# A two-layer diffusion backbone on one core: the FFN norm, the operand splits and the operand sums are emitted in turn with plain FFN tiles, the first two inner tiles are interleaved, and the next layer's modulation and norm are spread over the down phase

## The chip, the cores and the metric

The kernel runs on one core of a Trainium2 chip. The metric is the device time of one execution in microseconds (us), the median over several runs; less is better.

## The reference, cut to what matters

1024 latent tokens and 256 context tokens of width 1024 pass two layers. Everything is float32. What the change touches is the second half of a layer, its channel mixing, and the start of the next layer.

```python
def rms_norm(x, g, eps=1e-6):
    y = x * lax.rsqrt(jnp.mean(x * x, axis=-1, keepdims=True) + eps)
    return y * g
def swiglu(h, w_ffn_in, w_ffn_out):          # 1024 -> 2 x 2816 -> 1024
    gate, up = jnp.split(h @ w_ffn_in, 2, axis=-1)
    return (jax.nn.silu(gate) * up) @ w_ffn_out
...
for l in range(DEPTH):                       # DEPTH = 2
    mod_l = (jax.nn.silu(c) @ w_mod[l] + b_mod[l])[:, None, :]
    sh1, sc1, gt1, sh2, sc2, gt2 = jnp.split(mod_l, 6, axis=-1)
    h = rms_norm(x, g_norm1[l]) * (1.0 + sc1) + sh1
    ...                                      # attention, Fourier and GLA mixers -> mix
    x = x + gt1 * (mix @ w_out[l])
    h2 = rms_norm(x, g_norm2[l]) * (1.0 + sc2) + sh2
    x = x + gt2 * swiglu(h2, w_ffn_in[l], w_ffn_out[l])
```

## The kernel before, in words

**Arithmetic.** A float32 product is made of three fp32r matmuls (`mm3`, L166 to L169: high part by high part, high by low, low by high). Every operand, a weight or an activation, is split first (`split`, L161 to L163): ScalarE (ACT) casts the high part, VectorE (DVE) subtracts it for the low part. A 128x1024 weight comes by a DMA of 512 KB into a `raw` buffer (two of them, L141) and is split into `wh` and `wl`.

**Order.** The program is emitted by Python generators that `weave` takes in turn by paces; a scheduler then sets the order of each engine by the order of emission and the buffers that are free. On the chip each engine, and the DMA queue of SyncE (SP), runs its list strictly in order.

**Output projection and norm.** The latent tokens are handled in two halves of 512. `lat_early` does half 0: `wout`, the residual (L1077), the FFN's norm (`norm_raw`, with `norm_stats` L380 and the scaling L1087, L1088) and the splits of the eight 128x512 blocks. `lat_late` does half 1 and ends with its norm, its splits, and two of the operand sums (`combo`, L1144; "+" runs on DVE, "-" on GpSimd, which the profile calls POOL).

**First FFN product.** There are 22 inner tiles of 128 columns of gate and up. `ffn_plain` (L1161) makes one with 48 matmuls for each half, 96 in all. `ffn_seven` (L1184) makes one by a seven-product scheme over both halves, 84 matmuls: seven products named "11", "22", "1+", "4-", "3-", "7+", "6+" by their activation operand, 12 matmuls each; the weight sums come from POOL (L1205), and the results are collected in four tiles T1 to T4 (L1237 to L1256) of the buffer `XA`. The gated tile goes to DRAM (`gd`). `f0` tells how many tiles are plain: none in layer 0, 6 in layer 1.

**Next layer's modulation.** `next_mod` (L1051) makes 64 rows for layer 1: each loads 512 KB (`raw<-wmodT`, through the same two `raw` buffers) and reduces it against a vector on DVE (L327). Layer 0's `ffn_seven` emits three rows for each inner tile.

**Down phase.** For each half c = 0, 1 the second FFN product runs over f = 0 to 21: `down_tiles` loads a weight (`raw<-wff`, 512 KB) and a gated tile (`nx<-gd`, L1263), splits both, and `down_mm` runs 24 matmuls. Then L1332 adds the residual and L1333 stores. In layer 0, c = 1 starts with three tiles f (`LAG`), and then emits the whole of the next layer's first norm: `norm_stats`, and `norm1` (L471) with `norm_apply` (L408 to L410), 8 steps for the latent tokens and 8 for the context, ahead of the other 19 tiles.

Of the kernel before, what the change touches and what calls it, by code (L numbers as in the profile page):

```python
# [18 lines left out]
NC = 256  # L19
# [4 lines left out]
F0 = 6  # L24
FS = ("F", 20)
LAG = 3
NA = 6
# [16 lines left out]
class Prog:  # L44
# [374 lines left out]
    def layer(self, l):  # L419
# [9 lines left out]
        with tc.tile_pool(name=f"mix{l}", bufs=2, reuse_waits="tile") as mp:  # L429
# [16 lines left out]
            self.f0 = F0 if l else 0  # L446
# [4 lines left out]
            early = (f"early{l}", self.chain(*done, self.lat_early(l, lambda k: self.XA[:, k, :], self.f0)), PACE[f"early{l}"])  # L451
# [629 lines left out]
    def norm_raw(self, l, x):  # L1081

        nc = self.nc
        a2, sh2, _ = self.mods[l, "l", 1]
        nr = self.norm_stats(self.resident(x, 512), 512, False)
        for k in (4, 5, 6, 7, 0, 1, 2, 3):
# [9 lines left out]
    def lat_early(self, l, x, f0):  # L1096
# [3 lines left out]
        if f0:  # L1100
# [5 lines left out]
        if f0:  # L1106
            self.B["21"] = self.half(self.bp, ("H", 8))
        for k in range(4):
            self.split(x(k), *self.B["11"](k))
        if f0:  # L1110
            for k in range(4):
                self.split(x(k + 4), *self.B["21"](k))
        self.emitted.add((l, "early"))
        yield 10
        for f in range(f0):
            yield from self.ffn_plain(l, f, 0, False)

    def lat_late(self, l):
        X1 = [self.t(self.fp, [128, 2, 512], F32, *FS) for _ in range(4)]
        x = lambda k: X1[k // 2][:, k % 2, :]  # L1120
        act = self.lat_load(l, 1, x, self.fp, FS)
        yield PACE[f"late{l}"]
        yield from self.lat_proj(l, 1, act, x)
        yield from self.wait((l, "early"))
        self.norm_raw(l, x)
        self.raw1 = x
        B = self.B
        B["22"] = self.half(self.fp, FS)
        for k in range(4):
            self.split(x(k + 4), *B["22"](k))  # L1130
        if self.f0:
            B["12"] = self.half(self.fp, FS)
            for k in range(4):
                self.split(x(k), *B["12"](k))
        r = self.raw0
        self.combo("1+", self.fp, FS, lambda k: (r(k), x(k + 4), ALU.add))
        self.combo("4-", self.fp, FS, lambda k: (r(k + 4), r(k), ALU.subtract))

    def combo(self, name, pool, tag, parts):
        self.B[name] = self.half(pool, tag)  # L1140
        for k in range(4):
            a, b, op = parts(k)
            t = self.t(self.tp, [128, 512], F32, "nx", 3)[:]
            (self.nc.vector if "+" in name else self.nc.gpsimd).tensor_tensor(t, a, b, op)  # L1144
            self.split(t, *self.B[name](k))

    def combos2(self):
        r, x = self.raw0, self.raw1
        self.combo("3-", self.bp, ("H", 8), lambda k: (x(k), x(k + 4), ALU.subtract))
        self.combo("7+", self.fp, FS, lambda k: (r(k + 4), x(k + 4), ALU.add))  # L1150
# [34 lines left out]
    def ffn_seven(self, l, fs, fps):  # L1185
# [3 lines left out]
        self.wslot = 0  # L1189

        def weights(i):
            f, p = fs[i // 7], i % 7
# [22 lines left out]
        ev = self.t(self.bp, [128, 8, 512], F32, "XA", 1)  # L1215
        n = 7 * len(fs)
# [3 lines left out]
        for j, f in enumerate(fs):  # L1220
            if j % 2 == 0:
                bank = [self.t(fps, [128, 512], F32, "f", 4)[:] for _ in range(4)]
            else:
                bank = [self.mm_ps(), self.t_ps(), self.mm_ps(), self.t_ps()]
            T1, T2, T3, T4 = [ev[:, 4 * (j % 2) + z, :] for z in range(4)]
            for p in range(7):
                i = 7 * j + p
                if i + ahead < n:
                    weights(i + ahead)
                w, b = ws.pop(i), B[ops[p]]  # L1230
                ps = bank[(0, 1, 2, 0, 1, 2, 3)[p]]
                first, skip = p in (0, 1, 2, 6), p in (3, 4, 5)
                for k in range(4):
                    ks = slice(k * 128, (k + 1) * 128)
                    xh, xl = b(k)
                    self.mm3(ps, w[:, 0, ks], w[:, 1, ks], xh, xl, first and k == 0, k == 3, skip)
                if p == 0:  # L1237
                    nc.scalar.copy(T1, ps)
                elif p == 1:
                    tt(T2, T1, ps, ALU.add)  # L1240
                elif p == 2:
                    tt(T3, ps, T2, ALU.subtract)
                elif p == 3:
                    nc.scalar.copy(T4, ps)
                    tt(T2, T4, T2, ALU.subtract)
                elif p == 4:
                    self.last_silu = nc.scalar.activation(T1, ps, ACTF.Silu).ins
                    tt(T3, ps, T3, ALU.add)
                elif p == 5:
                    tt(T2, ps, T2, ALU.add)  # L1250
                    self.last_silu = nc.scalar.activation(T2, T2, ACTF.Silu).ins
                    tt(T2, T2, T4, ALU.mult)
                    self.gate_out(f, 0, T2)
                else:
                    tt(T3, ps, T3, ALU.add)
                    tt(T3, T3, T1, ALU.mult)  # L1256
                    self.gate_out(f, 1, T3)
            yield f
# [14 lines left out]
    def ffn_lat(self, l):  # L1273
# [5 lines left out]
        with tc.tile_pool(name=f"ffn{l}", bufs=2, reuse_waits="tile") as self.fp, \  # L1279
# [3 lines left out]
            self.weave(*self.bg)  # L1283
            self.bg = []
            self.mark(f"ffn{l}")
            for f in range(f0):
                drain(self.ffn_plain(l, f, 1, False))
# [19 lines left out]
            for c in range(2):  # L1307
# [10 lines left out]
                if c and not last:  # L1318
# [5 lines left out]
                    self.next_act = {"l": self.norm1(l + 1, "l", n, nr, self.resident(x0, n), False)}  # L1324
                    self.next_act["c"] = self.norm1(l + 1, "c", NC, nrc[:], self.streamed(self.xcsrc, 0, NC), True)
# [120 lines left out]
```

## Time and profile before

| | |
|---|---|
| three runs | 3105.53, 3109.64, 3114.30 us; median 3109.64 |
| the profiled execution's own time | 3104.48 us |
| its span in the trace | 3102.5 us |
| TensorE (PE) busy | 2809.1 us, 91% of the span, 13994 matmuls |
| DVE, ACT, POOL busy | 1936.0, 1346.2, 379.5 us |
| mean granted clock of TensorE | 0.95 |

The span is what the hardware profiler saw from the first to the last instruction of one execution; that execution's own time is 2 us longer. PE is the engine that a gap costs. The stages that the change touches lie, in that trace, at 985 to 1100 us (layer 0: end of `wout`, norm, splits, sums, first inner tiles), 1100 to 1479 (the rest of layer 0's `ffn_seven`), 1479 to 1670 (its down phase) and, in layer 1, 2456 to 2490 (norm, splits, sums) and 2553 to 2600 (the first inner tiles of `ffn_seven`).

### The profile page before, as it was taken

The numbers are of one execution on the slowest core, as the hardware profiler recorded it, in microseconds if no ns is written. First come the engines' busy times: TensorE is split into PE (matmuls) and PEld (weight loads), VectorE is DVE, ScalarE is ACT, GpSimd is POOL, SyncE is SP. The second block draws the span as 40 slices with busy tenths as digits, with TensorE's granted clock in tenths as the row PEclk, the third lists the DMA queues.
The fourth block names the chain that finished last, engine by engine and source line by source line (L and its number), as shares of the span: only waits on it lengthen the run. The fifth ranks groups of instructions, "written<-read, shape, count | busy, mean of one in ns | idle before, by whom it ended". The sixth has DMA issues, their size and how long they took to land. (4 is left out here: it accounts for less than half of the span.)

```text
span 3102.5 us, 38050 instructions
## 1 busy us (share of the span) xinstructions
PE 2809.1 (91%) x13994; PEld 2243.6 (72%) x13994; DVE 1936.0 (62%) x3061; ACT 1346.2 (43%) x2456; POOL 379.5 (12%) x278
## 2 busy tenths in 40 slices
PE   6999988989988789999996997996898899999999
PEld 3677676878876667777885876664676678888887
DVE  4266787877757887777435358686675566555342
ACT  3355565545545422322324256554445453333321
POOL 0000100000001333332000000010000024331000
PEclk9999997989999899999998999996898899999999
DMA  7754452424563254444635434434244322223642
GB/s 246 254 158 143 120 161 77 144 89 157 176 220 119 88 179 156 156 140 149 227 109 161 138 106 129 126 95 143 87 128 146 105 95 93 87 87 110 215 156 95
DMA packets 196890, 432.26 MB, mean 139 GB/s; under 512 B 23584, under 2 KB 59168, under 8 KB 195680
## 3 DMA queue, kind: packets, MB, share of 16 engines
q1 hardware_dynamic: 196704, 429.83, 42.9%
q8 instruction: 110, 1.80, 0.2%
q14 instruction: 76, 0.62, 0.1%
HBM read 357.65 MB, written 69.48 MB: 138 GB/s over the span
## 5 line engine op out<-in xcount | busy, mean ns | idle before, releaser
L163 DVE TENSOR_TENSOR wl<-raw,wh 128x1024 fp32r<-128x1024 f32 (+1 forms) x294 | 359.2, 1224 | 422.6 <-ACT wh L162 416.0
L162 ACT CAST wh<-raw 128x1024 fp32r<-128x1024 f32 (+2 forms) x303 | 309.0, 1023 | 545.1 <-PE t L168 278.5
L169 PE MATMUL mm<-H,wl 128*128 128x512 f32 x676 | 271.9, 404 | 0.0
L167 PE MATMUL mm<-H,wh 128*128 128x512 f32 x652 | 265.5, 409 | 4.1 <-ACT H L162 3.7
L168 PE MATMUL mm<-H,wh 128*128 128x512 f32 x652 | 262.1, 404 | 0.8 <-DVE H L163 0.8
L167 PE MATMUL f<-F,wh 128*128 128x512 f32 x468 | 184.8, 395 | 48.1 <-ACT F L162 48.1
L167 PE MATMUL mm<-F,wh 128*128 128x512 f32 x480 | 190.1, 396 | 19.6 <-ACT F L162 15.1
L168 PE MATMUL mm<-F,wh 128*128 128x512 f32 x480 | 190.8, 397 | 0.5 <-DVE F L163 0.5
L168 PE MATMUL f<-F,wh 128*128 128x512 f32 x468 | 184.1, 393 | 1.6 <-DVE F L163 1.6
L169 PE MATMUL f<-F,wl 128*128 128x512 f32 x468 | 184.5, 394 | 0.0
L169 PE MATMUL mm<-F,wl 128*128 128x512 f32 x456 | 180.2, 395 | 0.5 <-DVE wl L163 0.5
L167 PE MATMUL mm<-HC,wh 128*128 128x256 f32 x544 | 159.3, 294 | 1.9 <-DVE dcol L798 1.4
L168 PE MATMUL mm<-HC,wh 128*128 128x256 f32 x544 | 156.2, 288 | 0.6 <-DVE HC L410 0.3
L327 DVE CUSTOM_DVE_ANT_0 na<-raw,GC 128x1024 bf16<-128x1024 f32 x64 | 107.6, 1681 | 76.2 <-DMA raw<-wmodT 76.0
L169 PE MATMUL mm<-HC,wl 128*128 128x256 f32 x544 | 154.4, 285 | 0.8 <-DVE wl L163 0.8
L169 PEld LDWEIGHTS mm<-H,wl 128*128 128x128 f32 x676 | 129.7, 192 | 28.4 <-issue 2.8
L167 PEld LDWEIGHTS mm<-H,wh 128*128 128x128 f32 x652 | 124.5, 191 | 34.6 <-issue 5.5
L168 PEld LDWEIGHTS mm<-H,wh 128*128 128x128 f32 x652 | 124.5, 191 | 26.9 <-DVE H L163 1.7
L167 PEld LDWEIGHTS f<-F,wh 128*128 128x128 f32 x468 | 89.2, 191 | 68.0 <-ACT F L162 49.3
L672 ACT ACTIVATE P<-S,nm 128x640 f32<-128x640 f32 (+2 forms) x144 | 104.5, 731 | 71.0 <-DVE nm L668 70.3
L167 PEld LDWEIGHTS mm<-F,wh 128*128 128x128 f32 x480 | 91.6, 191 | 41.9 <-ACT F L162 17.0
L666 DVE TENSOR_REDUCE mx<-S 128x2 f32<-128x1280 f32 (+2 forms) x68 | 95.7, 1407 | 40.5 <-PE S L661 40.0
(581 smaller groups left out, 7166.2 us busy)
## 6 DMA issues: line engine op xcount, KB each, us to landing
raw<-wff SPq DMA_DIRECT2D x216, 512.0 KB, 3.7
raw<-wmodT SPq DMA_DIRECT2D x64, 512.0 KB, 3.6
raw<-wfm SPq DMA_DIRECT2D x52, 512.0 KB, 3.9
nx<-gd SPq DMA_DIRECT2D x88, 256.0 KB, 3.7
raw<-wout SPq DMA_DIRECT2D x40, 512.0 KB, 3.8
XC<-wff SPq DMA_DIRECT2D x38, 512.0 KB, 4.2
gd<-XA SPq DMA_DIRECT2D x76, 256.0 KB, 2.0
pt<-wmod SPq DMA_DIRECT2D x64, 256.0 KB, 4.6
```

What stands on the lines that cost most here:

```text
L162: self.nc.scalar.copy(hi, raw)
L163: (eng or self.nc.vector).tensor_tensor(lo, raw, hi.bitcast(F32), ALU.subtract)
L167: mm(ps, wh, xh, start=start, stop=False, skip_group_check=skip)
L168: mm(ps, wh, xl, start=False, stop=False, skip_group_check=skip)
L169: mm(ps, wl, xh, start=False, stop=stop, skip_group_check=skip)
L327: self.nc.vector.tensor_tensor_reduce(out=junk[:], in0=raw, in1=cs[s][:], op0=ALU.mult, op1=ALU.add, scale=1.0, scalar=0.0, accum_out=self ...
L666: nc.vector.tensor_reduce(mx[:, :nh], st[:, c0:c0 + nh * n].rearrange("p (a n) -> p a n", n=n), axis=AX.X, op=ALU.max)
L672: nc.scalar.activation(P[:, :n], st[:, c0 + z * n:c0 + (z + 1) * n], ACTF.Exp, bias=nm[:, hh:hh + 1], accum_out=sums[:, hh:hh + 1])
```

## The change

**Plain tiles.** `F0` becomes a pair for each layer: (0, 2) and (6, 1). The first number `fe` is the tiles that are plain and emitted early, as before (none, six); the second, `ff`, is new: plain tiles of which the first half is woven with the late norm, and the second half with the sums. So layer 0 has 2 plain tiles and 20 others (before 0 and 22), layer 1 has 7 and 15 (before 6 and 16). A plain tile has 12 matmuls more. Layer 0 now makes the splits B12 and B21 too, 8 more.

**Weaving.** The late norm and its splits are a generator (`late_norm`), as are the sums "1+", "4-", "3-" (`combos1`). "7+" and the operand of "6+" stay in `combos2`.

**Inner tiles.** `seq` sets the order of the products: the first tile's "7+" and "6+" come after the second tile's first three products. The first tile's T1 to T4 lie in buffers GC and HC; the others' in `XA` as before.

**Next layer's rows and norm.** Two rows are emitted for each inner tile of layer 0, 40 in all; the other 24 follow one for each f of the down phase's c = 0, and those left behind its last f. `norm1` is emitted one step for each f of c = 1. A side effect of `self.f0` being above zero in layer 0 is that its late half loads the mixers' output through `c1` (2 buffers), not `nx` (3).

```diff
-F0 = 6
+F0 = ((0, 2), (6, 1))
+REST = (32, 10)
...
-        self.norm_raw(l, x)
         self.raw1 = x
-        B = self.B
+    def late_norm(self, l):
+        B, x = self.B, self.raw1
+        yield from self.norm_raw_g(l, x)
         B["22"] = self.half(self.fp, FS)
         for k in range(4):
             self.split(x(k + 4), *B["22"](k))
-        if self.f0:
-            B["12"] = self.half(self.fp, FS)
-            for k in range(4):
-                self.split(x(k), *B["12"](k))
-        r = self.raw0
-        self.combo("1+", self.fp, FS, lambda k: (r(k), x(k + 4), ALU.add))
-        self.combo("4-", self.fp, FS, lambda k: (r(k + 4), r(k), ALU.subtract))
+            yield 1
+        B["12"] = self.half(self.fp, FS)
+        for k in range(4):
+            self.split(x(k), *B["12"](k))
+            yield 1
+    def combos1(self):
+        r, x = self.raw0, self.raw1
+        yield from self.combo("1+", self.fp, FS, lambda k: (r(k), x(k + 4), ALU.add))
+        yield from self.combo("4-", self.fp, FS, lambda k: (r(k + 4), r(k), ALU.subtract))
+        yield from self.combo("3-", self.bp, ("H", 8), lambda k: (x(k), x(k + 4), ALU.subtract))
...
+        seq = [(j, p) for j in range(len(fs)) for p in range(7)]
+        seq[5:10] = seq[7:10] + seq[5:7]
...
-            self.weave(*self.bg)
+            rest = [g for _, g, _ in self.bg] + [self.ffn_plain(l, f, 0, False) for f in range(self.fe, f0)]
-            for f in range(f0):
-                drain(self.ffn_plain(l, f, 1, False))
+            self.weave((f"norm{l}", self.late_norm(l), 20), (f"rest{l}", self.chain(*rest), REST[l]))
+            self.weave((f"comb{l}", self.combos1(), 12),
+                       (f"ffn{l}", self.chain(*[self.ffn_plain(l, f, 1, False) for f in range(f0)]), 10.2 * f0))
             self.combos2()
...
-                    for _ in range(3):
+                    for _ in range(2):
                         next(mod, None)
             if mod is not None:
-                drain(mod)
...
+                    step = self.chain(self.norm1(l + 1, "l", n, nr, self.resident(x0, n), False, True),
+                                      self.norm1(l + 1, "c", NC, nrc[:], self.streamed(self.xcsrc, 0, NC), True, True))
                 for f in range(len(lag), FT):
                     self.down_mm(ps, *self.down_tiles(l, f, c), f, range(KT))
+                    if not last:
+                        next(step if c else mod, None)
+                if not last:
+                    drain(step if c else mod)
```

What this does to the engines' lists is seen best at three places. Line numbers of the changed kernel stand a few higher (L354 for L353, L1094 for L1087, L164 for L163, L410 for L409).

DVE, layer 1, the norm of the late half, before: `na` is the norm's factor, L1087 scales the eight blocks of `F`, L163 makes low parts, L1144 a sum.

```order
L353 SCALAR_TENSOR_TENSOR na_19759<-t_19782,na_19759 128x512
L354 SCALAR_TENSOR_TENSOR na_19759<-na_19759,nacc_19758 128x512
L1087 SCALAR_TENSOR_TENSOR F_18803<-F_18803,a_1l_12594,na_19759 128x512 x2
L1087 SCALAR_TENSOR_TENSOR F_18804<-F_18804,a_1l_12594,na_19759 128x512 x2
L1087 SCALAR_TENSOR_TENSOR F_18801<-F_18801,a_1l_12594,na_19759 128x512 x2
L1087 SCALAR_TENSOR_TENSOR F_18802<-F_18802,a_1l_12594,na_19759 128x512 x2
L163 TENSOR_TENSOR F_19807<-F_18803,F_19805 128x512
```

The same place on DVE in the changed kernel; L164 `wl` is a weight's low part, and L575, L1189 and L1193 belong to the plain tile's activation.

```order
L354 SCALAR_TENSOR_TENSOR na_19803<-t_19826,na_19803 128x512
L355 SCALAR_TENSOR_TENSOR na_19803<-na_19803,nacc_19802 128x512
L164 TENSOR_TENSOR wl_19963<-raw_19960,wh_19962 128x1024
L1094 SCALAR_TENSOR_TENSOR F_18847<-F_18847,a_1l_13426,na_19803 128x512 x2
L575 SCALAR_TENSOR_TENSOR nx_19870<-nx_19871,nx_19870 128x512
L1094 SCALAR_TENSOR_TENSOR F_18848<-F_18848,a_1l_13426,na_19803 128x512 x2
L1189 TENSOR_TENSOR nx_19870<-nx_19871,nx_19870 128x512
L1094 SCALAR_TENSOR_TENSOR F_18845<-F_18845,a_1l_13426,na_19803 128x512 x2
L1094 SCALAR_TENSOR_TENSOR F_18846<-F_18846,a_1l_13426,na_19803 128x512
L1193 TENSOR_TENSOR nx_19870<-mm_19893,nx_19870 128x512
L1094 SCALAR_TENSOR_TENSOR F_18846<-F_18846,a_1l_13426,na_19803 128x512
L164 TENSOR_TENSOR F_19924<-F_18847,F_19922 128x512 x2
```

A plain tile's weight split and activation now stand between the scalings, which ran back to back before.

SP's DMA queue in layer 0's down phase, c = 0, before: only weights of the second product are left to load here.

```order
L141 DMA raw_13000<-wff 128x1024
L141 DMA raw_13035<-wff 128x1024
L141 DMA raw_13070<-wff 128x1024
L141 DMA raw_13105<-wff 128x1024
L141 DMA raw_13140<-wff 128x1024
```

The same stretch of SP's queue in the changed kernel; `wmodT` is a row of the next layer's modulation.

```order
L142 DMA raw_12949<-wff 128x1024
L142 DMA raw_12984<-wmodT 128x1024
L142 DMA raw_12988<-wff 128x1024
L142 DMA raw_13023<-wmodT 128x1024
L142 DMA raw_13027<-wff 128x1024
L142 DMA raw_13062<-wmodT 128x1024
```

Weights and rows now take the two `raw` buffers in strict turn.

ACT in layer 0's down phase, c = 1, before: L409 makes a block of the next layer's input (`HC`: the context's), `wh` and `F<-nx` are the casts for the down product; ahead of these rows stand L352, the norm's factor, and the eight steps for `H`.

```order
L409 ACTIVATE H_13540<-nx_13573,mod_1l 128x512
L409 ACTIVATE HC_13577<-nx_13581,mod_1c 128x256
L409 ACTIVATE HC_13577<-nx_13586,mod_1c 128x256
L162 CAST wh_13713<-raw_13711 128x1024
L409 ACTIVATE HC_13577<-nx_13591,mod_1c 128x256
L409 ACTIVATE HC_13577<-nx_13596,mod_1c 128x256
L409 ACTIVATE HC_13578<-nx_13601,mod_1c 128x256
L409 ACTIVATE HC_13578<-nx_13606,mod_1c 128x256
L409 ACTIVATE HC_13578<-nx_13611,mod_1c 128x256
L409 ACTIVATE HC_13578<-nx_13616,mod_1c 128x256
L162 CAST F_13649<-nx_13647 128x512
L162 CAST F_13684<-nx_13682 128x512
```

The same place on ACT in the changed kernel.

```order
L163 CAST F_13621<-nx_13619 128x512
L350 ACTIVATE nacc_13550<-t_13574,eps_87 128x512
L352 ACTIVATE nacc_13550<-nacc_13550 128x512
L353 ACTIVATE na_13551<-nacc_13550 128x512
L163 CAST wh_13615<-raw_13613 128x1024
L410 ACTIVATE H_13581<-nx_13648,mod_1l 128x512
L163 CAST wh_13654<-raw_13652 128x1024
L410 ACTIVATE H_13581<-nx_13687,mod_1l 128x512
L163 CAST F_13660<-nx_13658 128x512
L163 CAST wh_13693<-raw_13691 128x1024
L163 CAST F_13699<-nx_13697 128x512
```

Before, the first cast of a gated tile stood behind all sixteen steps; now the casts stand between them.

## Rows read from the trace of the kernel before

**Rows 1.** The page's first part: busy time of each engine.
```profile
PE 2809.1 (91%) x13994; PEld 2243.6 (72%) x13994; DVE 1936.0 (62%) x3061; ACT 1346.2 (43%) x2456; POOL 379.5 (12%) x278
```

**Rows 2.** Windows: length; PE, PEld, DVE, ACT, POOL busy (count); PEclk, DMA share, GB/s.
```profile
985.00:1100.00 115.00, 84.49 (x320) 64.92 (x319) 97.07 (x130) 52.16 (x90) 39.34 (x27) 0.84 0.33 110
1100.00:1479.00 379.00, 347.70 (x1485) 280.88 (x1484) 294.88 (x390) 112.23 (x200) 121.48 (x88) 0.98 0.45 153
1479.00:1579.00 100.00, 100.00 (x443) 82.84 (x442) 39.90 (x47) 34.14 (x44) 0.00 (x0) 1.00 0.58 194
1579.00:1670.00 91.00, 64.32 (x271) 51.80 (x270) 49.35 (x71) 34.31 (x49) 0.52 (x1) 0.85 0.41 135
2456.00:2490.00 34.00, 17.29 (x59) 12.37 (x58) 28.05 (x38) 20.52 (x34) 7.15 (x4) 0.74 0.12 39
2553.00:2600.00 47.00, 39.50 (x168) 32.30 (x167) 37.24 (x50) 21.77 (x37) 20.45 (x14) 0.93 0.30 100
2600.00:2700.00 100.00, 100.00 (x442) 82.80 (x442) 52.23 (x78) 33.93 (x58) 37.72 (x26) 1.00 0.25 85
```

**Rows 3.** Waits of PE, 985 to 1100: total us, times, longest us.
```profile
PE f L167 <- ACT F L162: 18.6, 2, 14.6
PE f L168 <- DVE F L163: 4.2, 2, 2.5
```

**Rows 4.** Waits of PE, 1100 to 1479.
```profile
PE f L167 <- DVE XA L1240: 14.2, 8, 2.9
PE t L167 <- DVE XA L1240: 11.0, 8, 1.5
```

**Rows 5.** Waits of DVE, 1100 to 1479.
```profile
DVE na L327 <- DMA raw<-wmodT: 74.7, 37, 5.4
```

**Rows 6.** Waits of PE, 1479 to 1670.
```profile
PE f L167 <- ACT F L162: 25.9, 1, 25.9
```

**Rows 7.** Waits of PE, 2553 to 2600.
```profile
PE f L167 <- ACT F L162: 7.5, 1, 7.5
```

**Rows 8.** Groups of DVE, 1249.6 to 1291.8: busy us, mean ns, idle before.
```profile
L327 DVE CUSTOM_DVE_ANT_0 na<-raw,GC 128x1024 bf16<-128x1024 f32 x6 | 11.0, 1834 | 9.1 <-DMA raw<-wmodT 9.1
L1252 DVE TENSOR_TENSOR XA<-XA 128x512 f32<-128x512 f32 x2 | 3.6, 1820 | 0.2
...
L1245 DVE TENSOR_TENSOR XA<-XA 128x512 f32<-128x512 f32 x2 | 1.4, 687 | 0.0
```

**Rows 9.** SP's queue in order of time, 1249 to 1272: start, us.
```profile
1250.21 12.22 SPq L141 DMA_DIRECT2D raw<-wmodT  x3
```

**Rows 10.** Groups of DVE, 985 to 1048.
```profile
L163 DVE TENSOR_TENSOR F<-nx,F 128x512 fp32r<-128x512 f32 x12 | 11.0, 952 | 0.0
```

**Rows 11.** POOL in order of time, 1010 to 1030.
```profile
1014.14 4.98 POOL L1144 TENSOR_TENSOR nx<-XA 128x512 f32<-128x512 f32 x3 [1.46 <-DVE F L163]
```

**Rows 12.** Groups of all engines, 1479 to 1579 (down phase, c = 0).
```profile
L163 DVE TENSOR_TENSOR wl<-raw,wh 128x1024 fp32r<-128x1024 f32 x17 | 20.8, 1225 | 43.1 <-ACT wh L162 43.1
L162 ACT CAST wh<-raw 128x1024 fp32r<-128x1024 f32 x18 | 18.9, 1051 | 47.7 <-PE t L168 47.7
```

**Rows 13.** The page's DMA issues: count, KB each, median us to landing.
```profile
raw<-wff SPq DMA_DIRECT2D x216, 512.0 KB, 3.7
raw<-wmodT SPq DMA_DIRECT2D x64, 512.0 KB, 3.6
```

**Rows 14.** DVE in order of time, 1615 to 1660.
```profile
1626.41 0.69 DVE L353 SCALAR_TENSOR_TENSOR na<-t,na 128x512 f32<-128x512 f32 x1 [6.89 <-ACT na L352]
...
1655.40 0.69 DVE L163 TENSOR_TENSOR F<-nx,F 128x512 fp32r<-128x512 f32 x1 [2.00 <-ACT F L162]
```

**Rows 15.** SP's queue in order of time, 1640 to 1670.
```profile
1651.97 12.61 SPq L1263 DMA_DIRECT2D nx<-gd  x10
```

**Rows 16.** PE in order of time, 2456 to 2480.
```profile
2456.81 0.39 PE L169 MATMUL mm<-F,wl 128*128 128x512 f32 x1
...
2473.22 1.22 PE L167 MATMUL mm<-F,wh 128*128 128x512 f32 x2 [12.02 <-ACT F L162]
```

**Rows 17.** DVE in order of time, 2456 to 2492.
```profile
2464.73 5.39 DVE L1087 SCALAR_TENSOR_TENSOR F<-F,a_1l,na 128x512 f32<-128x512 f32 x8
```

**Rows 18.** ACT in order of time, 2456 to 2492.
```profile
2471.01 3.73 ACT L162 CAST F<-F 128x512 fp32r<-128x512 f32 x7
```

More of the change, by code (lines that the diff above doesn't have):

```diff
@@ L450, in layer @@
             done = [self.wait((l, z)) for z in ("lgla", "fft", 3)]
-            early = (f"early{l}", self.chain(*done, self.lat_early(l, lambda k: self.XA[:, k, :], self.f0)), PACE[f"early{l}"])
+            early = (f"early{l}", self.chain(*done, self.lat_early(l, lambda k: self.XA[:, k, :])), PACE[f"early{l}"])
             if l == 0:
@@ L1081, in norm_raw, with norm_raw_g @@
     def norm_raw(self, l, x):
+        for _ in self.norm_raw_g(l, x):
+            pass
+    def norm_raw_g(self, l, x):
         nc = self.nc
@@ L1105, in lat_early @@
         self.B["11"] = self.half(self.bp, ("H", 8))
-        if f0:
-            self.B["21"] = self.half(self.bp, ("H", 8))
+        self.B["21"] = self.half(self.bp, ("H", 8))
         for k in range(4):
             self.split(x(k), *self.B["11"](k))
-        if f0:
-            for k in range(4):
-                self.split(x(k + 4), *self.B["21"](k))
+        for k in range(4):
+            self.split(x(k + 4), *self.B["21"](k))
         self.emitted.add((l, "early"))
         yield 10
-        for f in range(f0):
+        for f in range(self.fe):
             yield from self.ffn_plain(l, f, 0, False)
@@ L1214, in ffn_seven @@
         ops = ["11", "22", "1+", "4-", "3-", "7+", "6+"]
-        ev = self.t(self.bp, [128, 8, 512], F32, "XA", 1)
-        n = 7 * len(fs)
+        e1 = self.t(self.bp, [128, 2, 512], F32, "GC", 1)
+        e2 = self.t(self.bp, [128, 2, 512], F32, "HC", 4)
+        first = [e1[:, 0, :], e1[:, 1, :], e2[:, 0, :], e2[:, 1, :]]
+        ev = None
+        n = len(seq)
         ahead = 3
@@ L1219, in ffn_seven @@
             weights(i)
-        for j, f in enumerate(fs):
-            if j % 2 == 0:
-                bank = [self.t(fps, [128, 512], F32, "f", 4)[:] for _ in range(4)]
-            else:
[L1224 to L1258, printed above, removed]
@@ new lines, in ffn_seven @@
+        tiles = {}
+        for i, (j, p) in enumerate(seq):
+            f = fs[j]
+            if p == 0:
+                if j % 2 == 0:
+                    bank = [self.t(fps, [128, 512], F32, "f", 4)[:] for _ in range(4)]
+                else:
+                    bank = [self.mm_ps(), self.t_ps(), self.mm_ps(), self.t_ps()]
+                if j == 1:
+                    ev = self.t(self.bp, [128, 8, 512], F32, "XA", 1)
+                tiles[j] = bank, [ev[:, 4 * (j % 2) + z, :] for z in range(4)] if j else first
+            bank, (T1, T2, T3, T4) = tiles[j]
+            if i + ahead < n:
+                weights(i + ahead)
+            w, b = ws.pop(i), B[ops[p]]
+            ps = bank[(0, 1, 2, 0, 1, 2, 3)[p]]
+            new, skip = p in (0, 1, 2, 6), p in (3, 4, 5)
+            for k in range(4):
+                ks = slice(k * 128, (k + 1) * 128)
+                xh, xl = b(k)
+                self.mm3(ps, w[:, 0, ks], w[:, 1, ks], xh, xl, new and k == 0, k == 3, skip)
+            if p == 0:
+                nc.scalar.copy(T1, ps)
+            elif p == 1:
+                tt(T2, T1, ps, ALU.add)
+            elif p == 2:
+                tt(T3, ps, T2, ALU.subtract)
+            elif p == 3:
+                nc.scalar.copy(T4, ps)
+                tt(T2, T4, T2, ALU.subtract)
+            elif p == 4:
+                self.last_silu = nc.scalar.activation(T1, ps, ACTF.Silu).ins
+                tt(T3, ps, T3, ALU.add)
+            elif p == 5:
+                tt(T2, ps, T2, ALU.add)
+                self.last_silu = nc.scalar.activation(T2, T2, ACTF.Silu).ins
+                tt(T2, T2, T4, ALU.mult)
+                self.gate_out(f, 0, T2)
+            else:
+                tt(T3, ps, T3, ALU.add)
+                tt(T3, T3, T1, ALU.mult)
+                self.gate_out(f, 1, T3)
+                yield f
```

23 lines of the change are left out of this document (13 added, 10 removed).

## The prediction

> **What bounds the kernel now.** I read the busy times first, then windows laid over the stages that the change touches, then the waits of PE in each, and last the order of time around each gap. PE is busy 2809.1 us, 91% of the span, no other engine over 62% [rows 1]: what is to be had is PE's gaps and its stretches at the lower clock, and added matmuls cost in full. A matmul of 128x512 at full clock takes 100/442 = 0.226 us (the window at 2600 [rows 2]). So each window's loss is its length less 0.226 us for each matmul [rows 2]: layer 0's norm, sums and first tiles 115 - 320 x 0.226 = **42.6**; the rest of its seven-product tiles 379 - 1485 x 0.226 = **43.1**; down phase c = 0 nothing (443 in 100 us); its second half and c = 1's start 91 - 271 x 0.226 = **29.7**; layer 1's norm 34 - 59 x 0.226 = **20.7**; its first seven-product tiles 47 - 168 x 0.226 = **9.0**. Together 145 us. In the windows with long gaps the granted clock is below 1 (0.74, 0.84 and 0.85): part of each ran at the lower level, 1.2 GHz, after PE had stood still. So a gap costs more than its length, and that share leaves with it.
>
> What ends the gaps: in the first, casts and low parts of the sums' operands [rows 3]; in the second, DVE's L1240 [rows 4], which is late because DVE itself waits 74.7 us for rows of the modulation [rows 5]; in the down phase one single wait of 25.9 us for a cast [rows 6]; in layer 1 the norm chain [rows 16] and the "7+" operand [rows 7].
>
> **The change part by part.** Everything is worked out against the profiled execution, 3104.48 us (span 3102.5); the median of the three runs shown lies 5.2 us above it.
>
> *Layer 0, 985 to 1100.* The norm chain of the late half, from its last residual to the low parts, is some 23 us (two waits of 18.6 and two of 4.2 [rows 3]). Now the first-half matmuls of two plain tiles, 96 x 0.226 = 21.7 us, lie beside it: I leave 2 us. Then 96 second-half matmuls, again 21.7 us, lie beside the sums. DVE has there four adds (0.69 as L1245 [rows 8]), twelve splits that took 0.952 instead of 0.69 us beside POOL's sums [rows 10], four weight splits of 1.225 [rows 12] and six activation operations (0.69): 2.8 + 11.4 + 4.9 + 4.1 = 23 us. DVE is as long as PE, and "7+" and "6+" follow; the swap of products gives these three products of the second tile (36 x 0.226 = 8.1 us) as cover. I leave 6 us. So 42.6 becomes 8: -34.6. Two plain tiles have 24 matmuls more: +5.4. Net **-29**. The mix load in 2 buffers instead of 3 holds SP back a little: **+2** (0 to 6).
>
> What speaks against this part is POOL beside DVE. The row pair shows it: an operation on two buffers takes 1820 ns where POOL works and 687 where it doesn't [rows 8], 1.13 us more. The Trainium skill (SBUF — State Buffer, section SBUF: two separate sides) says that a DVE operation with two SBUF inputs and a GpSimd operation that reads SBUF take an exclusive lock, so that the later one waits the whole instruction out. The pair agrees. By the rule each of the eight POOL sums, 1.66 us (4.98 / 3 [rows 11]), would be added whole: 13 us, where the mean of the twelve splits gives 12 x 0.26 = 3. The sum would then be 10 us worse.
>
> *Layer 0, 1100 to 1479.* The window holds 18 inner tiles (1485 / 84). DVE is busy 294.9 / 18 = 16.4 us in each [rows 2] and waits 74.7 / 18 = 4.2 for rows [rows 5]: 20.6 of the 21.1 us that a tile takes, where PE needs 84 x 0.226 = 19.0. The rows come slowly because three loads are issued in turn as the two buffers come free (12.22 us for three [rows 9]) and a DVE row that waits holds all behind it. With two rows DVE has 16.4 - 1.83 [rows 8] = 14.6, and two waits at 74.7 / 54 = 1.4 each: 17.4, under 19.0. PE bounds. I keep 9 us for the start, where the first row waits for GC, now T1 and T2 of the first tile, and for late tiles: **-34**. If each of the two rows waited as long as now three do together, DVE would need 18.8, still under PE; a little jitter then costs some 15.
>
> *Down phase, c = 0.* Twenty-four rows come here. Each is a load of 512 KB on SP and 1.83 us on DVE, which is busy only 39.9 of 100 us [rows 2, 8]. Bounds: nothing (the loads have the time: a weight lands in 3.7 us, a row in 3.6 [rows 13], PE needs 24 x 0.226 = 5.43 for one f), and a full series on two buffers that take strict turns: weight 3.7, cast 1.05, low part 1.23 [rows 12], row 1.83, its load 3.6, together 11.4 us for an f. ACT waits 47.7 us in this window for PE [rows 12], so weights are ready early today and have slack. Nearest to what the order makes is a weight's own buffer cycle, 3.7 + 1.05 + 1.23 and some handing over, 6.0 to 6.6 us, while the row's load runs beside it. At 6.4 that is 22 x 0.97 = 21 us, less two tiles ahead (10.9; `wh` and `wl` have three buffers each): **+10** (0 to 30). The Trainium skill (DMA: Bandwidth & Descriptors, Specifications) gives one core 358 GB/s from HBM; the 194 GB/s here [rows 2] plus 524 kB in 5.43 us, 97 GB/s, make 291. By that limit alone the rows would be free, and the sum 10 us better.
>
> *Down phase, c = 1.* PE stands still from 1629 to 1655 because the first cast of a gated tile is behind sixteen norm steps, which run from 1627 to 1653 on DVE [rows 14]; the tile's own load, 12.61 us of issue for ten, starts at 1652 only [rows 15]. Now each f carries one step: two DVE operations of about 0.7 us (as L353 [rows 14]) and one on ACT, beside a low part of 1.23 and one of 0.69: 3.3 of 5.43 us. It fits. What stays is the norm's factor (DVE waits 6.9 us for it [rows 14]), which the three lag tiles and the first cast now cover, the last rows and the modulation's last sums between the evictions: 6 us. 29.7 becomes 6: **-24**.
>
> *Layer 1, norm.* The chain is 16.4 us long (2456.8 to 2473.2 [rows 16]), 5.4 of it scaling on DVE [rows 17] and 3.7 casts on ACT [rows 18]. One plain tile's 48 first-half matmuls, 10.9 us, now lie beside it. But its two weight splits and its activation stand between the scalings on DVE and ACT: two of 1.23 and five of about 0.7, 6 us. The chain grows to 22.4, 11.5 stay open, and the clock falls as now: **-5**, less 12 more matmuls (+2.7): **-2** (-8 to +3).
>
> *Layer 1, 2553.* The wait of 7.5 us for "7+" [rows 7] gets 8.1 us more cover: **-8**.
>
> *Sum.* -29 + 2 - 34 + 10 - 24 - 2 - 8 = -85: 3019.5 us for an execution like the profiled one, 3024 (with the 5.2) for a median.
>
> **Rivals.**
> 1. *The two raw buffers bind the down phase harder*, 7.5 to 8 us an f: 22 x 2.3 = 51, 41 more than my 10. Time 3065. For it: two buffers, strict turns. Against it: ACT's 47.7 us of slack [rows 12].
> 2. *DVE stays the bound of the first stretch*: each POOL sum (1.66 us [rows 11]) holds it up whole, 13 - 3 = 10 us more, and the rows still jitter (10 to 15). Time 3047. For it: the slowed operations [rows 8, 10]. Against it: most splits beside POOL were slowed by less [rows 10].
> 3. *The change does little where PE had cover already*: the list before put some "11" products ahead of the stats, and ACT and DVE work of the plain tiles eats what the matmuls cover. Half of -29, -2 and -8 is lost: 3044.
> 4. *Slower.* The row on DVE stands behind a weight's low part, which waits for PE, and the next weight's load stands behind the row's on SP: the series of 11.4 us becomes the pace of c = 0. 22 x (11.4 - 5.43) = 131 against the 95 that the other parts give: 36 slower, 3146. It decides from 5.43 + 95/22 = 9.75 us an f. Against it: DVE is idle half of the stage and a row needs nothing of PE.
>
> **How the numbers follow.** My forecast 0.62, rival 1 0.13, rival 2 0.11, rival 3 0.10, rival 4 0.04. The likeliest time is 3024. The range goes down to 2985: rows free (-10), no rest in the first two windows (-17), layer 1's norm at its better bound (-6), c = 1 clean (-6). It goes up to 3070, past rivals 1 to 3. A measurement of this kernel tells about 0.3%, 9 us, from no change. Rivals 1 to 3 are faster by far more: faster 0.93; within 0.3%, a down phase of about 9.5 us an f, 0.03; slower 0.04.
>
> **What would show it.** The window of 1100 to 1479 has no PE wait for L1240 of note and DVE's waits for rows are about half. The single wait of 25.9 us is gone, and casts of gated tiles stand between norm steps. c = 0 shows some 10 us of PE waits for `wh` or `wl`, or none. Layer 1 keeps a wait of some 11 us for the cast of `F`. I am wrong if c = 0 loses over 30 us, if the sums leave PE waiting over 15 us ahead of "7+", or if the c = 1 gap only moves to its end.

## The result

The changed kernel takes 3054.86 us in the median of four runs (3048.44 to 3061.03), the kernel before 3107.59 (3102.23 to 3114.30): ratio 0.9829, 95% interval 0.9800 to 0.9858, about 53 us faster. The forecast was 3024, 85 faster, with a range of 2985 to 3070. So the direction and the range held, and 32 us of the forecast gain did not come.

The profiled execution of the changed kernel took 3055.01 us with a span of 3052.9; PE is busy 2821.7 us, 92%. Its windows, with the columns of [rows 2], cut where the stages now end:

```profile
985.00:1133.00 148.00, 127.35 (x509) 100.80 (x508) 121.55 (x154) 76.83 (x130) 49.53 (x32) 0.93 0.34 115
1133.00:1456.00 323.00, 318.00 (x1384) 259.26 (x1383) 251.80 (x329) 103.54 (x183) 102.92 (x75) 1.00 0.45 146
1456.00:1596.00 140.00, 126.31 (x529) 98.53 (x527) 66.96 (x95) 34.50 (x42) 0.00 (x0) 0.99 0.69 222
1596.00:1720.00 124.00, 123.07 (x535) 101.15 (x536) 70.50 (x95) 49.16 (x69) 0.53 (x1) 0.99 0.53 172
```

The second line is 1384 matmuls in 323 us, nearly PE's own pace (313). The down phase's c = 0, 120 us before, is now 140 long for the same matmuls. The first still holds 33 us of loss.

To compare kernels whose stages lie at other times, I put the split matmuls of both traces (10056 before, 10092 after) in order, since their number up to a stage is known, and took from each stage's length 0.226 us for each matmul; what is left is the stage's loss. This ledger is worked out of the traces, no view prints it:

| stage (us lost) | before | after | forecast |
|---|---|---|---|
| layer 0, 985 us and the next 336 matmuls (norm, sums, first tiles) | 44.2 | 24.8 | 8 (to 1100 us) |
| the next 168 matmuls | 10.8 | 9.3 | |
| the other seven-product tiles | 32.5 | 10.1 | 9 (from 1100 us) |
| length of down phase c = 0 | 119.7 | 140.2 | 130 |
| length of c = 1 | 149.9 | 123.1 | 126 |
| layer 1, around the norm | 23.0 | 12.0 | 15.7 (of 20.7) |
| layer 1, first seven-product tiles | 9.2 | 8.5 | 1 (of 9.0) |

The forecast of 9 is for all that lies behind 1100 us, the last 1537 matmuls ahead of the down phase: these lose 43.4 us before and 19.3 after. From 985 us to the down phase it is 506.3 and 471.0 us: 35.3 less (61 forecast), with 24 matmuls more. Then +20.5 (+10 forecast), -26.8 (-24), and in layer 1 -11.7 with 12 matmuls more (+2.7), -9.0 (-10): together -50.6 (-85). The spans differ by 49.6; the rest, 1 us, is scatter in stages that the change leaves alone.

What PE waits for in the first of these windows, after (columns as in [rows 3]):

```profile
PE t L396 <- DVE nacc L394: 4.7, 2, 4.5
PE f L168 <- DVE GC L1263: 4.1, 1, 4.1
PE f L168 <- ACT GC L1261: 3.8, 1, 3.8
PE mm L168 <- ACT XA L1261: 3.0, 1, 3.0
```

The waits of [rows 3], casts and low parts, are gone. In their place stand the context's norm statistics (L394), and the first tiles' T1 and T2 (L1261, L1263) in the new buffer GC. In the second window DVE's wait for rows is nearly what it was, first before (1154 to 1491 us, the same matmuls), then after:

```profile
DVE na L327 <- DMA raw<-wmodT: 69.6, 32, 5.4
```

```profile
DVE na L328 <- DMA raw<-wmodT: 68.3, 34, 4.6
```

And in the down phase the pace of c = 0 can be read off SP's queue (start, us, loads):

```profile
1547.32 0.33 SPq L142 DMA_DIRECT2D raw<-wff  x1
1548.47 0.33 SPq L142 DMA_DIRECT2D raw<-wmodT  x1
1553.27 0.33 SPq L142 DMA_DIRECT2D raw<-wff  x1
1554.42 0.33 SPq L142 DMA_DIRECT2D raw<-wmodT  x1
1559.21 0.33 SPq L142 DMA_DIRECT2D raw<-wff  x1
```

A weight every 5.94 us here; the next one took 7.61, and the mean over the 22 f is 6.4 (140.2 / 22), where PE wants one every 5.43. In c = 1 the wait of 25.9 us [rows 6] has gone, and casts stand between the steps:

```profile
1614.74 1.06 ACT L163 CAST wh<-raw 128x1024 fp32r<-128x1024 f32 x1 [1.55 <-PE t L169]
1615.70 0.72 ACT L410 ACTIVATE H<-nx,mod_1l 128x512 fp32r<-128x512 f32 x1
1616.32 1.03 ACT L163 CAST wh<-raw 128x1024 fp32r<-128x1024 f32 x1
1617.26 0.72 ACT L410 ACTIVATE H<-nx,mod_1l 128x512 fp32r<-128x512 f32 x1
1617.88 0.61 ACT L163 CAST F<-nx 128x512 fp32r<-128x512 f32 x1
```

### The profile page after: what moved, and what is told of

Same layout as the page of the kernel before. It is cut to its first block, busy times and chain, and to the rows that moved or that the text cites. A ratio compares the mean times of both kernels' runs of the same rounds, so it can differ in the third digit from the quotient of the medians.

```text
span 3052.9 us, 38121 instructions
## 1 busy us (share of the span) xinstructions
PE 2821.7 (92%) x14030; PEld 2249.8 (74%) x14030; DVE 1930.1 (63%) x3054; ACT 1356.7 (44%) x2474; POOL 353.7 (12%) x263
## 5 line engine op out<-in xcount | busy, mean ns | idle before, releaser
L164 DVE TENSOR_TENSOR wl<-raw,wh 128x1024 fp32r<-128x1024 f32 (+1 forms) x306 | 373.2, 1222 | 395.5 <-ACT wh L163 378.1
L163 ACT CAST wh<-raw 128x1024 fp32r<-128x1024 f32 (+2 forms) x315 | 321.3, 1024 | 541.0 <-PE mm L169 202.6
L168 PE MATMUL mm<-H,wh 128*128 128x512 f32 x700 | 284.1, 408 | 4.1 <-ACT H L163 3.7
L170 PE MATMUL mm<-H,wl 128*128 128x512 f32 x712 | 284.7, 401 | 0.0
L169 PE MATMUL mm<-H,wh 128*128 128x512 f32 x700 | 281.6, 404 | 0.8 <-DVE H L164 0.8
L168 PE MATMUL mm<-F,wh 128*128 128x512 f32 x520 | 205.2, 395 | 10.9 <-ACT F L163 9.9
L169 PE MATMUL mm<-F,wh 128*128 128x512 f32 x520 | 205.8, 396 | 1.2 <-DVE F L164 1.2
L170 PE MATMUL mm<-F,wl 128*128 128x512 f32 x508 | 200.8, 396 | 1.0 <-DVE wl L164 1.0
L168 PE MATMUL f<-F,wh 128*128 128x512 f32 x452 | 178.8, 396 | 12.6 <-ACT wh L163 6.7
L169 PE MATMUL f<-F,wh 128*128 128x512 f32 x452 | 177.9, 394 | 0.0
L168 PEld LDWEIGHTS mm<-H,wh 128*128 128x128 f32 x700 | 133.2, 191 | 36.4 <-issue 5.5
L169 PEld LDWEIGHTS mm<-H,wh 128*128 128x128 f32 x700 | 133.3, 191 | 29.5 <-issue 2.1
L328 DVE CUSTOM_DVE_ANT_0 na<-raw,GC 128x1024 bf16<-128x1024 f32 x64 | 93.0, 1453 | 82.2 <-DMA raw<-wmodT 78.6
L696 PE MATMUL t<-ident,P 128*128 128x128 f32 x640 | 110.4, 288 | 10.9 <-DVE P L689 4.7
```

Of the source, the lines that this page charges most:

```text
L163: self.nc.scalar.copy(hi, raw)
L164: (eng or self.nc.vector).tensor_tensor(lo, raw, hi.bitcast(F32), ALU.subtract)
L168: mm(ps, wh, xh, start=start, stop=False, skip_group_check=skip)
L169: mm(ps, wh, xl, start=False, stop=False, skip_group_check=skip)
L170: mm(ps, wl, xh, start=False, stop=stop, skip_group_check=skip)
L328: self.nc.vector.tensor_tensor_reduce(out=junk[:], in0=raw, in1=cs[s][:], op0=ALU.mult, op1=ALU.add, scale=1.0, scalar=0.0, accum_out=self ...
```

## The experiments

Runs with one time each are compared by the ledger of their traces, since whole times scatter by some 6 us. "The stretch" is from the 985 us point to layer 0's down phase; the changed kernel loses 44.2 us in it (24.8 + 9.3 + 10.1). Three of the runs below have the same code up to its end (the rows in XC, the norm at once, six plain tiles in layer 1) and lose 42.6, 41.1 and 41.5. So a difference there is good to some 3 us, and the trace that the others are compared with is the highest of the four. In the same way, six traces with the same code in layer 1 lose 5.7 to 8.5 us in its first seven-product tiles, and the changed kernel's is at the upper end.

### Which of three causes holds the first tiles up

**The sums on DVE.**

```diff
-            (self.nc.vector if "+" in name else self.nc.gpsimd).tensor_tensor(t, a, b, op)
+            self.nc.vector.tensor_tensor(t, a, b, op)
```

> The changed kernel with the sums 4- and 3- on DVE instead of POOL. Its stretch from 985 us to the first matmul of layer 0's down phase takes 471.0 us and loses 44.2, of which 34 lie before 1133. Theory A (POOL's operand sums lock DVE out): eight adds of 0.69 us come to DVE, the low parts of 1.7 us beside them go back to 0.69, and the stretch becomes 6 to 10 us shorter. Theory B (DVE and ACT only have too much queued ahead of the first tile's results, whatever POOL does): 0 to 4 us longer, since DVE has 5.5 us more to do. Theory C (the context's norm in the middle of the first tiles): no change beyond 2 us.

Measured: 3042.67 us; the stretch loses 36.2, 8.0 less (5 to 8 against the four traces), and layer 1's first tiles lose 2.4 instead of 8.5 (5.7 to 8.5). Some groups of DVE from 1020 to 1060, first the changed kernel, then this one:

```profile
L164 DVE TENSOR_TENSOR F<-nx,F 128x512 fp32r<-128x512 f32 x11 | 8.5, 785 | 3.1 <-ACT F L163 3.0
L164 DVE TENSOR_TENSOR H<-nx,H 128x512 fp32r<-128x512 f32 x4 | 5.3, 1326 | 1.3 <-ACT H L163 1.2
L1165 DVE TENSOR_TENSOR XA<-XA,F 128x512 f32<-128x512 f32 x4 | 4.8, 1228 | 0.0
...
L1189 DVE TENSOR_TENSOR nx<-nx,nx 128x512 f32<-128x512 f32 x2 | 2.3, 1156 | 0.1
```

```profile
L164 DVE TENSOR_TENSOR F<-nx,F 128x512 fp32r<-128x512 f32 x11 | 7.3, 681 | 1.8 <-ACT F L163 1.8
...
L164 DVE TENSOR_TENSOR H<-nx,H 128x512 fp32r<-128x512 f32 x4 | 2.7, 686 | 2.9 <-ACT H L163 2.9
...
L1165 DVE TENSOR_TENSOR XA<-XA,F 128x512 f32<-128x512 f32 x4 | 2.7, 678 | 0.0
...
L1189 DVE TENSOR_TENSOR nx<-nx,nx 128x512 f32<-128x512 f32 x2 | 1.4, 686 | 2.4 <-ACT nx L576 2.4
```

In the order of time the means come apart: of the changed kernel's 39 TENSOR_TENSOR operations of 128x512 in these 40 us, ten take 1.1 to 1.8 us and the other 29 take 0.68 or 0.69; with the sums on DVE all 47 take 0.67 to 0.69, although eight more are there. The ten cost DVE 10 us, and the eight adds 5.4. Theory A holds, but the run moves two things at once. In the changed kernel ACT's casts also wait for POOL's sums themselves, and less for the same sums on DVE (first the changed kernel, from 1020 to 1060 us, then this one):

```profile
ACT F L163 <- POOL nx L1156: 6.4, 4, 3.0
ACT H L163 <- POOL nx L1156: 4.2, 4, 1.7
```

```profile
ACT F L163 <- DVE nx L1156: 4.8, 5, 1.9
...
ACT H L163 <- DVE nx L1156: 1.0, 2, 0.6
```

How much of the gain is DVE's slowed operations and how much the later sums, no run takes apart.

**The last sums later.** `combos2()` moves from ahead of `ffn_seven` into it:

```diff
-            self.combos2()
...
+            if i == 3:
+                self.combos2()
```

> The changed kernel with the last sums (7+ and the operand of 6+) emitted after the first inner tile's third product instead of ahead of the first. Theory B (they stand ahead of the first tile's results on ACT and DVE, so that PE waits 4.2 and 4.7 us for T1 and T2): both waits go, 8 to 12 us less with the clock that they cost. Theory A (the lock): within 3 us, the same operations beside the same POOL sums. Theory C: within 2 us.

Measured: 3049.83 us, but the stretch loses 43.5 (0.7 less). The wait for T1 became longer, not shorter:

```profile
PE f L168 <- ACT GC L1263: 8.4, 1, 8.4
PE t L396 <- DVE nacc L394: 7.0, 1, 7.0
```

So Theory B falls for layer 0: the wait for T2 has gone from the list, but the two that are left are longer. In layer 1, which the edit changes too, the order does count: there the wait for T1 stays (2.1 us), the one for T2 falls, and the first tiles lose 3.2 us instead of 5.7 to 8.5. The T2 wait there, first the changed kernel, then this one:

```profile
PE f L168 <- DVE GC L1263: 3.0, 1, 3.0
```

```profile
PE f L168 <- DVE GC L1265: 0.5, 1, 0.5
```

**The context's statistics later.** The two lines of `nrc` move into the loop over `ffn_seven`, at its fourth tile.

```diff
+                if f == f0 + 3 and not last:
+                    nrc = self.t(self.tp, [128, NC], F32, "nrc", 1)
+                    nc.vector.tensor_copy(nrc[:], self.norm_stats(self.streamed(self.xcsrc, 0, NC), NC, True))
```

> The changed kernel with the context's norm statistics emitted after the fourth inner tile instead of ahead of the first. Theory C (they stand in the way: PE waits 4.9 us for their sum, ACT loads tables four times): 7 to 10 us less, most of it in 1066 to 1081. Theories A and B: the time only moves to the next late result, within 3 us.

Measured: 3046.15 us; the stretch loses 37.8, 6.4 less, all in its first 336 matmuls (17.1 for 24.8, with 1.3 back in the next). Some 3 us come back where the statistics now stand: the 300 matmuls from the sixth tile on lose 4.4 us, in the four traces 0.8 to 1.3. So the stretch gains less than the expected 7 to 10 (3 to 6 against the four traces), but where the statistics stood C holds too. In the changed kernel ACT changed tables around that norm:

```profile
1073.25 1.28 ACT L350 ACT_TABLE_LOAD   x1
1076.35 0.47 ACT L350 ACTIVATE nacc<-t,eps 128x256 f32<-128x256 f32 x1 [1.82 <-PE t L396]
1076.84 1.28 ACT L1274 ACT_TABLE_LOAD   x1
...
1078.79 1.28 ACT L352 ACT_TABLE_LOAD   x1
```

### The down phase's two buffers

```diff
-                self.mod_row(l, s, r, self.load_raw(self.wmodT[l - 1, r]), cs)
+                if self.rowxc:
+                    raw = self.t(self.bp, [128, 1024], F32, "XC", 2)[:]
+                    nc.sync.dma_start(raw, self.wmodT[l - 1, r])
+                else:
+                    raw = self.load_raw(self.wmodT[l - 1, r])
+                self.mod_row(l, s, r, raw, cs)
```

> The changed kernel with the 24 rows of the down phase loaded into the two XC buffers, which nothing uses there, instead of the two raw buffers. It takes 140.2 us from the first matmul of c = 0 to the first of c = 1, against 119.7 in the kernel before. Theory D (strict turns on two buffers set the pace): 120 to 123 us, and the whole 17 to 20 us shorter. Rival (the link, or SP's queue, or DVE sets the pace): over 130 us.

Measured: 3025.98 us. c = 0 as a whole, and its part up to the last row's load:

```profile
1455.60:1575.30 119.70, 119.70 (x530) 99.15 (x529) 62.76 (x85) 36.15 (x45) 0.00 (x0) 1.00 0.72 246
1455.60:1512.00 56.40, 56.40 (x250) 46.74 (x249) 39.87 (x57) 20.35 (x26) 0.00 (x0) 1.00 0.92 321
```

PE is busy all 119.7 us at 246 GB/s. Not all rows lie in it: with buffers of their own they run ahead, so that 16 of the 64 are reduced inside c = 0, where the changed kernel has 21. But 14 of them are loaded in the first 56 us, one in 4 us, faster than one for each f, and PE is busy there too, at 321 GB/s. So Theory D holds to the whole 20.5 us; link, SP and DVE had room. The other 8.5 us of this one time are spread over stages that the edit leaves alone.

### Parts undone

**The norm at once.**

```diff
-                    step = self.chain(self.norm1(l + 1, "l", ...), self.norm1(l + 1, "c", ...))
+                    step = drain(self.chain(self.norm1(l + 1, "l", ...), self.norm1(l + 1, "c", ...)))
+                step = iter(())
```

> The changed kernel with the next layer's norm emitted all at once again in c = 1 of layer 0's down phase. It takes 123.1 us from the first matmul of c = 1 to the first after it, against 149.9 in the kernel before. Theory (the sixteen steps ahead of the first cast are the whole wait): about 149 us again and the whole 24 to 27 slower. Rival (the split loads or the rows took part of it): under 140.

Measured: 3086.35 us; c = 1 takes 151.2, 28.1 more. The wait is back:

```profile
PE f L168 <- ACT F L163: 24.8, 1, 24.8
```

**Three rows for each tile.**

```diff
-                    for _ in range(2):
+                    for _ in range(3):
                         next(mod, None)
             if mod is not None:
+                drain(mod)
```

> The changed kernel with three rows of the modulation for each inner tile again, the last four ahead of the down phase, none in it. Theory (DVE's queue with three waited rows is what bounds the seven-product tiles): the stretch from the 505th matmul after 985 to the down phase, 322.9 us with a loss of 10.1, loses 25 to 32 again, c = 0 takes 119.7 instead of 140.2, and the whole is within 5 us of the changed kernel. Rival (the loss went with the plain tiles or the swap, rows don't matter): the stretch stays at 323 and the whole is 20 us shorter.

Measured: 3060.50 us. That stretch, 322.9 us in the changed kernel, takes 356.1 and loses 43.2, more than expected (25 to 32), and c = 0 takes 120.1. So the 24 rows cost 33 us there (the third of each tile and the four behind the last tile, which this run doesn't part), and 20 in c = 0.

**No plain tile in layer 0.**

```diff
-F0 = ((0, 2), (6, 1))
+F0 = ((0, 0), (6, 1))
```

> The changed kernel with no plain tile in layer 0 (22 seven-product tiles, the rest as changed). Theory (the two plain tiles cover the norm chain of some 20 us): PE waits 14 us and more for the first cast again, the stretch from 985 to the down phase loses 62 to 70 us instead of 44, and with 24 matmuls less (5.4 us) the whole is 13 to 20 us slower. Rival (the cover is eaten by the plain tiles' own ACT and DVE work): within 5 us of the changed kernel.

Measured: 3063.22 us, 8 more than the changed kernel, under the expected 13. The stretch loses 60.7, 16.5 more, so the cover is real; less 5.4 for the matmuls that is 11. c = 0 took 135.0 there instead of 140.2: with 22 such tiles 44 of the 64 rows go with them, and 17 instead of 21 are reduced in c = 0. At 20.5 / 24 us a row, four rows would be 3.4 us of the 5.2, an estimate.

**No swap of products.**

```diff
-        seq[5:10] = seq[7:10] + seq[5:7]
```

> The changed kernel without the swap of products between the first two inner tiles (both layers). In it layer 1's first 84 matmuls around the first seven-product tile lose 8.5 us, 9.2 in the kernel before. Theory E (the swap does give 7+ its cover, but the first tile's T1 and T2, which ACT and DVE write behind the sums, are a new wait): without it PE waits for both, 6 to 10 us more in layer 1, as much in layer 0, the whole 8 to 18 us slower. Rival F (the swap covers nothing): within 3 us in both layers.

Measured: 3040.93 us, faster. Layer 1's first tiles lose 8.4, as with the swap, and layer 0's stretch loses 38.4, 5.8 less (3 to 6 against the four traces). Of the 14 us of the whole the rest lies where nothing changed. So E falls; F holds in layer 1, and in layer 0 the swap costs some 3 to 6 us. PE's waits there, without it:

```profile
PE f L168 <- ACT F L163: 5.0, 1, 5.0
PE f L168 <- ACT GC L1260: 3.8, 1, 3.8
PE t L396 <- DVE nacc L394: 2.6, 1, 2.6
```

The wait for T1 is the same 3.8 us; the one for T2 (4.1) is traded for one of 5.0, which ends when the first cast of `F<-XA` is done. That is the operand of "6+", since the other sums are split from `nx`.

**Six plain tiles in layer 1.**

```diff
-F0 = ((0, 2), (6, 1))
+F0 = ((0, 2), (6, 0))
```

> The changed kernel with six plain tiles in layer 1 as before, none beside the norm. Around that norm it loses 12.0 us where the kernel before lost 23.0. Theory G (48 matmuls cover the chain, and the plain tile's own work doesn't lengthen it): 22 to 24 us lost there again, 12 matmuls less (2.7 us), the whole 7 to 10 slower. Rival (the splits of the late half in two parts made the gain): within 3 us.

Measured: 3060.76 us. Around the norm it loses 19.3 us (12.0 with the seventh tile, 23.0 before), and the first tiles 6.2 (8.5). G holds for two thirds: the tile gives 7.3, and after 2.7 for its matmuls 4.6 are left. The other 3.7 came with the weaving of the splits and sums, which no run takes apart. The first tiles' 6.2 is no sign of this edit: it lies within the 5.7 to 8.5 of the same code.

### Put together

**Three edits.** The diffs of the sums on DVE, the context's statistics later, and the XC buffers, in one kernel.

> The changed kernel with three edits together: 4- and 3- on DVE, the context's norm statistics after the fourth inner tile, the down phase's rows in the XC buffers. If the three losses are separate (8.0, 6.4 and 20.5 us in the stretches of the single runs), the stretch from 985 to the down phase loses about 30 us, c = 0 takes 119.7, and the whole is some 35 us under the changed kernel, near 3020. If two of them hide the same wait, the stretch loses 34 or more.

Measured: 3021.03 us. c = 0 takes 120.8, but the stretch loses 42.4, not 30: its first 336 matmuls 15.6, the next 168 11.2 and the last part 15.6 instead of 10.1. By the bound set down beforehand (34 or more) the losses are not separate: the first two edits give 7 us where they act, not 14, and 5 are lost again behind. For those 5 the next run tries this: the statistics, moved there, meet a DVE that two rows keep at PE's pace. Why the first 504 matmuls gave only half is open. Layer 1 gained 9.8 us, about 6 of it in the first seven-product tiles (2.4 us lost for 8.5).

**One row for each tile, one for each f of both halves.** Only the first 32 rows are needed by the next norm.

```diff
-                    for _ in range(2):
+                    for _ in range(1):
                         next(mod, None)
...
-                        next(step if c else mod, None)
-                if not last:
-                    drain(step if c else mod)
+                        next(mod, None)
+                        if c:
+                            next(step, None)
+                if c and not last:
+                    drain(step)
+                    drain(mod)
```

> The kernel of the three edits with one row of the modulation for each inner tile, and one for each f in both halves of the down phase (XC buffers). In the run of the three edits the stretch from the 505th matmul after 985 to the down phase loses 15.6 us, c = 0 takes 120.8 us and c = 1 152.5 to its 528th matmul and on to the next stage. Theory (DVE with two rows for a tile is just at PE's pace, so every added operation, as the moved statistics, shows): the loss falls to 3 to 8 us, c = 0 and c = 1 stay within 2 us, the whole is 8 to 14 under the three edits. Rival (POOL's weight sums bound that stretch): no change there.

Measured: 3008.96 us. The stretch from the 505th matmul loses 1.1, less than the 3 to 8 expected; PE is busy all of it:

```profile
1123.70:1437.70 314.00, 314.00 (x1387) 260.04 (x1386) 203.26 (x305) 112.97 (x189) 110.20 (x75) 1.00 0.39 130
```

POOL works there as much as before, so it did not bound that stretch. DVE's waits for rows fell to 23.7 us, and it now waits for PE too:

```profile
DVE na L328 <- DMA raw<-wmodT: 23.7, 15, 2.8
...
DVE XA L1270 <- PE mm L170: 8.6, 7, 1.4
DVE XA L1270 <- PE f L170: 8.2, 6, 1.4
```

**The same without the swap.**

> The kernel of the three edits with one row for each inner tile and each f, and without the swap of products. Timed in three rounds as the best version so far. If the swap's cost in layer 0 (5.7 us between 985 and the down phase in the single run without it) doesn't hang on the sums on POOL or the statistics, it comes off here too: about 3003 us, ratio to the kernel before about 0.966. If it was made by those, 3007 to 3010, ratio 0.968.

Measured, in three rounds: 3004.82 us in the median (2999.35 to 3006.25), the kernel before 3106.55; ratio 0.9665, interval 0.9644 to 0.9686. This beats both kernels, some 50 us under the changed one. The median lies between the two expectations. In the profiled execution the stretch loses 20.8 us, with the swap it was 25.4: 4.6 less, so the swap's cost seems to come off here too, as far as two single traces that scatter by 3 us tell.

## Why the prediction was right, and where it was wrong

- **The direction and the largest terms.** PE's gaps were the thing to be had, and one of the three large ones went as worked out: c = 1 by 26.8 us (24 forecast), which the norm at once gave back. The seven-product tiles behind 1100 us went the right way, as the third row shows, but from 43.4 to 19.3 and not to 9. That 3054.86 lies inside the range is owed to its width: of the 32 us that are missing, some 26 are lost between 985 us and the down phase and 10 in c = 0, and c = 1 gave 3 more than forecast.
- **Wrong: "I leave 6 us" for the sums** in *Layer 0, 985 to 1100*. The norm chain is covered: the stretch loses 1.5 us up to 1024. But from there to 1133 the sums and the first tiles lose 32.6. PE waits 11.1 us from 1024 to the first of the products "7+" and "6+" and 15.6 to the second (4.5 of it for the context's statistics), so the 15 us that I had named as a sign of being wrong were as good as reached. I had counted DVE's work (23 us against 21.7) with 3 us for POOL beside it, and that is where the step failed: POOL's sums were worth 5 to 8 us by their run, and the context's statistics, which I had not counted at all because before they lay inside other waits, 3 to 6. That PE waits for T1 and T2 in their new place was not in the sum either. By the rule of the Trainium skill (SBUF — State Buffer, section SBUF: two separate sides) that my prediction set beside the row, the sum was to be 10 us worse. The trace agrees more with it than with my mean over twelve splits: ten operations of DVE took 1.1 to 1.8 us, 10 us more than at 0.68. What the rest hangs on stays open: the last version, without operand sums on POOL, the statistics' old place, the swap and the second row, still loses 20.8 us in the stretch.
- **Right for a wrong reason: the rows.** I wrote that two rows would wait 1.4 us each, and that DVE's waits would halve. They are 34 waits of 2.0 us, 68.3 in all: my second case, in which two rows wait as long as three did (18.8 us a tile), is what came. What was enough is that DVE does one row less in each tile: 15.3 us of work by the window (251.8 us in 1384 / 84 tiles) and 4.1 of waiting, 19.4 of the 19.6 that a tile takes, where PE needs 19.0. It is still the bound, by 0.6 us a tile: so the moved statistics showed at once, and only one row for each tile took the rest off.
- **Mis-sized: the two raw buffers, "+10".** The pace was the one that I took from the rows, 6.4 us for an f in the mean. But I took 10.9 us off for tiles that are ready ahead, and c = 0 gained nothing from them: 15 us of loss inside it, and 5.4 more at the start of c = 1, where the last rows are loaded through the same buffers ahead of its first weights. Rival 1 had the place right, but not its 7.5 to 8 us an f. The sentence beside it on the bandwidth of one core (the Trainium skill, DMA: Bandwidth & Descriptors, Specifications) said that the rows would be free. The trace of the XC run agrees that the link had that room, 321 GB/s in its first 56 us with PE never idle. The buffers took it away.
- **Layer 1, two errors that cancel.** The norm was to give 2 us net and gave 8.3: the plain tile's operations did stand between the eight scalings, which now stretch over 7.2 us instead of 5.4, but the first casts began among them, so that the chain from the last residual's matmul to PE's next product is 19 us long, not 22.4 (16.4 before). The "7+" wait was to give 8, and the stage gave 0.7 (0.7 to 3.5 with the other traces of the same code). That the two sum up to about the forecast is luck. I had also misread [rows 7]: the wait of 7.5 us ended with a cast of `F<-XA`, the operand of "6+".

```profile
2561.59 0.80 PE L167 MATMUL f<-F,wh 128*128 128x512 f32 x1 [7.50 <-ACT F L162]
```

```profile
2560.92 1.13 ACT L162 CAST F<-XA 128x512 fp32r<-128x512 f32 x2
```

The swap moves "6+" as well as "7+", and that wait has gone. But two waits for T1 and T2 came in its place, 2.1 and 3.0 us and the clock that they cost, and they are the same there without the swap. With the sums on DVE that stage loses 2.4, the wait for T1 is gone and T2's is 2.0, so most of it was POOL's sums again.
- **The mix load** (+2) was not tried by itself. By 985 us the changed kernel is 12 matmuls (2.7 us) behind, but runs of the same code differ there by up to 46, so this shows nothing.
- **The slower rival** did not come near: c = 0 took 6.4 us an f in the mean, where it needed 9.75.

## What to carry to other kernels

Work that is moved to fill a stage brings its buffers along: ask which ring it loads through, and give it one that is idle there, before asking whether the link or the engine has room. Beside a busy DVE, a sum on POOL is not free, and eight of them on DVE itself can be cheaper than the same eight beside it. Work emitted "somewhere near", as a small norm whose result is needed 500 us later, should stand where the engines have slack, since in an engine's list it holds everything up that is behind it.

## What was not expected of the hardware

Beside POOL's sums it is single operations of DVE that grow, and not all of them a little: between 1020 and 1060 us ten of 39 took 1.1 to 1.8 us, nine of them over 1.6, and 29 their usual 0.68 or 0.69. A mean, such as the prediction's 952 ns over twelve, hides that. And c = 0 had the DMA queues at 222 GB/s in the mean with PE waiting, but with two more buffers at 321 in its first 56 us without a wait: which buffers the loads took in turn was what counted, not the sum of the loads.
